# First Fourier mixer of an encoder trunk: chunk-wise shift, a first projection block that follows the chunks, and the gate's slice of the conditioning placed two blocks later

## The chip, the cores and the metric

The kernel runs on one core of one Trainium2 chip. The time is the device time of one launch in microseconds (us). A core has five engines that take their instructions in the order of the program: TensorE (PE in the rows below, with its weight loads as PEld), VectorE (DVE), ScalarE (ACT), GpSimd (POOL) and SyncE (SP), which here issues nearly all DMA transfers.

## The reference, cut to what matters

Two layers of a mixer and a channel mixer are applied to 768 tokens (512 of one group, 256 of another, each with a conditioning vector c) of width 1024. The change touches only the first mixer of layer 0, which in the reference is:

```python
mod = (cs @ ada_w[layer] + ada_b[layer])[:, None, :]      # cs = silu(c)
sh1, sc1, g1, sh2, sc2, g2 = jnp.split(mod, 6, axis=-1)
h = rmsnorm(x, norm_mix_g[layer]) * (1.0 + sc1) + sh1
hf = h.astype(jnp.float32).reshape(bsz, s, FNET_GROUPS, FNET_GROUP_DIM)
mixed = jnp.fft.fft2(hf, axes=(1, 3), norm='ortho').real.reshape(bsz, s, d).astype(h.dtype)
y = mixed @ fnet_w + fnet_b
x = x + g1 * y
```

So a Fourier transform over the sequence and over each group of 128 features, a projection 1024 x 1024, and a gated residual. Six vectors of 1024 per sequence (scale, shift and gate of the two halves of the layer) come from one product each with a slice of `ada_w`. A shift is constant along the sequence, so the transform over the sequence puts it on frequency 0 alone.

## The kernel before, in words

The work is float32. A plain float32 matmul stands in the profile's counts as two entries, so "x24" of such rows is 12 instructions. The projections run as three float32r products (high x high, low x high, high x low): weights and activations are split into a high part (cast on ACT, `wh`, `hh`) and a low part (subtraction on DVE, `wl`, `hl`).

The first mixer handles the features in 8 chunks of 128 (KC = 8). Its steps, with their lines:

- **Slices of the conditioning** (`ada_steps`, L242 to L268). A slice is 8 loads of 512 KB into tiles `at`, of which there are three (`apool`, bufs=3), each followed by four narrow matmuls into `sm`; then a copy `av`, two transposes and an addition give `modT`. Called "a group" below: the four matmuls of one load. Slice 1 is the scale, 0 the shift, 2 the gate; 4 and 3 belong to the next half of the layer.
- **Transform over the sequence** (L709 to L725): per chunk 12 float32 matmuls into a two-bank tile `big` of a pool with three buffers, then a copy to `xt` on ACT and DVE.
- **Scale and shift** (L732 to L737): `xt` times the scale on ACT and POOL, and the shift added to the two zero frequencies on DVE. This needs slices 1 and 0, so both stand before the transforms in the program.
- **Transform over the features** (L738 to L745): two matmuls per chunk, copies to `cs_` on ACT.
- **Mixing** (L746 to L756): cosine and sine parts combined on DVE and POOL to `mx`, then split to `hh` and `hl` (L195, L196).
- **Projection** (L757 to L770): for each of 8 blocks of 128 outputs, `load_block` and 24 matmuls of 512 columns and 24 of 256 (8 chunks x 3 products), in a PSUM pool `ppr` with six banks. The residual of a block (L482) multiplies by the gate, so it needs slice 2; after each block, `advance(steps, 3)` takes three steps of slices 4 and 3. The blocks are called m0 to m7 here.

The framework's scheduler sets each engine's order from the program's order as priority, and moves later work ahead where it expects the earlier work to wait. The split weights have five buffers for `wh` and five for `wl`, each half a block; the loaded weights (`stg`) have six.

Of the kernel before, what the change touches and what calls it, by code (L numbers as in the profile page):

```python
# [12 lines left out]
F32 = mybir.dt.float32  # L13
# [7 lines left out]
P = 128  # L21
# [19 lines left out]
YW = 512  # L41
PAIRS = (1, 3, 5)
ST = 4
SGB = 3
M7 = 2
WP = 5
# [59 lines left out]
def encoder_kernel(  # L106
# [87 lines left out]
    def split_to(ah, al, src, eng=None):  # L194
        A_.copy(ah, src)  # L195
        (eng or V).tensor_tensor(al, src, ah.bitcast(F32), ALU.subtract)  # L196
# [72 lines left out]
    def ada(*args):  # L269
        for s in args[0]:  # L270
            yield from ada_steps(s, *args[1:])

    def advance(gen, n=1000):
        for _ in range(n):
            if next(gen, gen) is gen:
                break
# [379 lines left out]
    with ExitStack() as l0:  # L656
# [5 lines left out]
        weights["av"] = l0.enter_context(tc.tile_pool(name="avp", reuse_waits="tile", bufs=1))  # L662
        ap0 = l0.enter_context(ExitStack())
        apool = ap0.enter_context(tc.tile_pool(name="apool", reuse_waits="tile", bufs=3))
        with ExitStack() as fs:
            pbig = fs.enter_context(tc.tile_pool(name="pbig0", reuse_waits="tile", bufs=3, space=PSUM))
            fp = fs.enter_context(tc.tile_pool(name="fp", reuse_waits="tile", bufs=1))
            wk = fs.enter_context(tc.tile_pool(name="fwk", reuse_waits="tile", bufs=2))
            ld, *rows = load_rows(wk)
            pairs = ((0, 2), (1, 3), (4, 5))  # L670
            xt = [fp.tile([P, D], F32, name="xt", bufs=8) for j in range(NT)]
            ftab = fp.tile([P, FCOLS], F32, name="ftab")
            for i, pair in enumerate(pairs):
                for j in pair:
                    nc.sync.dma_start(xt[j], x_prompt[0, j * P : (j + 1) * P, :] if j < 4 else x_sample[0, (j - 4) * P : (j - 3) * P, :])
                if i == 0:
                    nc.sync.dma_start(ftab, tab_d[:, :FCOLS])
            even = [fp.tile([P, D], F32, name=f"even{i}") for i in range(3)]
            odd = [fp.tile([P, D], F32, name=f"odd{i}") for i in range(3)]
            for i, (a, b) in enumerate(pairs):  # L680
                ss = wk.tile([P, 2], F32, name="ss")
                with tc.issue_after(ld.ins):
                    for n, (j, scratch) in enumerate(((a, even[i]), (b, odd[i]))):
                        A_.activation(scratch, xt[j], AF.Square, accum_out=ss[:, n : n + 1])
                    A_.activation(ss, ss, AF.Ln, bias=eps, scale=1.0 / D)
                    A_.activation(ss, ss, AF.Exp, scale=-0.5)
                xb = odd[i]
                V.tensor_scalar(xb, xt[b], ss[:, 1:2], None, ALU.mult)
                V.scalar_tensor_tensor(even[i], xt[a], ss[:, 0:1], xb, ALU.mult, ALU.add)
                V.scalar_tensor_tensor(odd[i], xt[a], ss[:, 0:1], xb, ALU.mult, ALU.subtract)  # L690
                for j in (a, b):
                    pt = pbig.tile([P, 1024], F32, name="big")
                    for c in range(KC):
                        last = nc.tensor.transpose(pt[:, c * P : (c + 1) * P], xt[j][:, c * P : (c + 1) * P], ident)
                    (XC[j] and A_.copy or V.tensor_copy)(xa[:, :, j * P : (j + 1) * P], pt.rearrange("p (c i) -> p c i", i=P))
                if i == 0:
                    with tc.issue_after(last.ins):
                        setup_c(psm, rows[0])
            with tc.issue_after(last.ins):
                setup_rows(psm, *rows[1:])  # L700

            NC, NS = S0 // 2 + S1 // 2 + 2, S0 // 2 + S1 // 2 - 2
            pcs = []
            advance(ada((1,), psm, apool))
            make_amod(0)
            advance(ada((0,), psm, apool))
            for c in range(KC):
                pcs.append(fp.tile([P, NC + NS], F32, name="xt", bufs=8))
                ps = pbig.tile([P, 1024], F32, name="big")  # L709
                oc, os_ = 0, 512  # L710
                for g, s in ((0, S0), (1, S1)):
                    for par in (0, 1):
                        ncs = s // 4 + 1 - par
                        nsn = s // 2 - ncs
                        nkt = s // 2 // P
                        for kt in range(nkt):
                            o, n = COLS[f"seq{g}_{kt}_{par}"]
                            src = (odd if par else even)[2 if g else kt][:, c * P : (c + 1) * P]
                            fl = dict(start=(kt == 0), stop=(kt == nkt - 1))
                            mm(ps[:, oc : oc + ncs], src, ftab[:, o : o + ncs], **fl)  # L720
                            mm(ps[:, os_ : os_ + nsn], src, ftab[:, o + ncs : o + n], **fl)
                        oc += ncs
                        os_ += nsn
                A_.copy(pcs[c][:, :NC], ps[:, :NC])
                V.tensor_copy(pcs[c][:, NC:], ps[:, 512 : 512 + NS])  # L725
            shs = fp.tile([P, KC, 2], F32, name="shs")
            for g, s in ((0, S0), (1, S1)):
                V.tensor_scalar(shs[:, :, g : g + 1], modT[:, 0, :, g : g + 1], float(s / math.sqrt(s * P)), None, ALU.mult)

            c1, s1 = S0 // 2 + 1, NC + S0 // 2 - 1  # L730
            for c in range(KC):
                y = pcs[c]  # L732
                for g, (lo, hi) in enumerate(((0, c1), (c1, NC))):
                    A_.activation(y[:, lo:hi], y[:, lo:hi], AF.Copy, scale=amod[:, 0, c, g : g + 1])
                for g, (lo, hi) in enumerate(((NC, s1), (s1, NC + NS))):
                    G.tensor_scalar(y[:, lo:hi], y[:, lo:hi], amod[:, 0, c, g : g + 1], None, ALU.mult)
                V.tensor_tensor(y[:, 0 : c1 + 1 : c1], y[:, 0 : c1 + 1 : c1], shs[:, c], ALU.add)  # L737
                pf = pbig.tile([P, 1024], F32, name="big")  # L738
                o, n = COLS["cosd"]
                mm(pf[:, 0:NC], ftab[:, o : o + n], y[:, :NC])  # L740
                o, n = COLS["sind"]
                mm(pf[:, 512 : 512 + NS], ftab[:, o : o + n], y[:, NC:])
                cs_ = wk.tile([P, NC + NS], F32, name="cs_")
                A_.copy(cs_[:, NC:], pf[:, 512 : 512 + NS])
                A_.copy(cs_[:, :NC], pf[:, :NC])  # L745
                mx = wk.tile([P, T], F32, name="mx")  # L746
                for lo, s, ec, es in ((0, S0, 0, NC), (S0, S1, c1, s1)):
                    q, h = s // 4, s // 2
                    V.tensor_copy(mx[:, lo : lo + h + 1 : h], cs_[:, ec : ec + q + 1 : q])
                    for eng, op, ev, od in (  # L750
                        (V, ALU.subtract, slice(lo + 2, lo + h, 2), slice(lo + 1, lo + h, 2)),
                        (G, ALU.add, slice(lo + s - 2, lo + h, -2), slice(lo + s - 1, lo + h, -2)),
                    ):
                        eng.tensor_tensor(mx[:, ev], cs_[:, ec + 1 : ec + q], cs_[:, es : es + q - 1], op)
                        eng.tensor_tensor(mx[:, od], cs_[:, ec + q + 1 : ec + h + 1], cs_[:, es + q - 1 : es + h - 1], op)
                split_to(hh[c], hl[c], mx)  # L756
        with ExitStack() as fs:  # L757
            fp = fs.enter_context(tc.tile_pool(name="fp2", reuse_waits="tile", bufs=1))
            ppr = fs.enter_context(tc.tile_pool(name="ppr0", reuse_waits="tile", bufs=6, space=PSUM))
            advance(ada((2,), psm, apool))  # L760
            steps = ada((4, 3), psm, apool)
            gb = fp.tile([P, KC, 2], F32, name="gb")
            V.tensor_tensor(gb, modT[:, 2], gT[:, 40:48].unsqueeze(2).to_broadcast([P, KC, 2]), ALU.mult)
            for m in range(KC):
                po = product(ppr, load_block(fnet_w[0], 0, KC, m * P), hh, hl, KC)
                for g, (lo, ln) in enumerate(SEGS):
                    A_.activation(xs[m][:, lo : lo + ln], xs[m][:, lo : lo + ln], AF.Identity, bias=gb[:, m, g : g + 1])
                residual(xs[m], po, 2, m)
                advance(steps, 3)
        ap0.close()  # L770
        with ExitStack() as fs:
            wk = fs.enter_context(tc.tile_pool(name="wk0", reuse_waits="tile", bufs=1))
# [586 lines left out]
```

## Time and profile before

| | us |
|---|---|
| median of 3 timed runs | 1894.94 (1893.63 to 1900.61) |
| the profiled execution's own time | 1897.02 |
| its span, first to last instruction | 1895.30 |
| PE busy | 1803.9 (95%) |
| DVE busy | 1422.9 (75%) |
| ACT busy | 975.1 (51%) |
| POOL busy | 501.5 (26%) |
| mean granted TensorE clock | 0.989 of full speed |

The chain that ended last is 66% PE over the span. The first mixer takes the first 156 us: slices and sequence transforms until 52.7 us, feature transforms and mixing until 75.0 us, the eight blocks after that. A granted clock of 1.00 is the higher of TensorE's two levels (2.4 GHz), 0.50 the lower (1.2 GHz).

### The profile page before, as it was taken

How to read it: one execution, taken by the hardware profiler on the slowest of the kernel's cores; microseconds unless marked ns; L12 is line 12 of the kernel's file. 1: busy time of each engine (PE TensorE's matmuls, PEld its weight loads, DVE VectorE, ACT ScalarE, POOL GpSimd, SP SyncE). 2: the span in 40 equal slices, each digit the busy share in tenths (PEclk: the TensorE clock that was granted, in tenths of full speed). 3: DMA queues.
4: the chain of work that ended last, by engine and by line, in shares of the span. 5: the costliest groups of instructions: out<-in, count | busy, mean ns of one | idle time of the engine just before them, and what ended most of it. 6: DMA issues, size and time to landing. Idle time of an engine off the chain costs nothing.

```text
span 1895.3 us, 29959 instructions
## 1 busy us (share of the span) xinstructions
PE 1803.9 (95%) x11317; PEld 1642.6 (87%) x11317; DVE 1422.9 (75%) x2431; ACT 975.1 (51%) x1863; POOL 501.5 (26%) x417
## 2 busy tenths in 40 slices
PE   8899899999999999999999999989899999999998
PEld 6587888999999987888888888778699999999997
DVE  4637777777686767897787787783788888889875
ACT  3626544444454435856666556652564554555543
POOL 1400132333332320123213213221103334343431
PEclk9999999999999999999999999999899999999999
DMA  8842344343434344322222221141312222222211
GB/s 275 245 168 67 123 134 131 109 139 110 147 112 156 112 153 151 116 51 64 64 53 66 68 64 58 53 150 39 86 34 83 84 68 68 67 70 82 72 45 67
DMA packets 221546, 189.72 MB, mean 100 GB/s; under 512 B 19152, under 2 KB 199513, under 8 KB 221401
## 3 DMA queue, kind: packets, MB, share of 16 engines
q1 hardware_dynamic: 220992, 187.66, 32.4%
q8 instruction: 89, 1.46, 0.3%
q14 instruction: 56, 0.46, 0.1%
q10 hardware_dynamic: 409, 0.15, 0.0%
HBM read 174.36 MB, written 13.42 MB: 99 GB/s over the span
## 4 chain that ended last, share of the span: by engine, by line
PE 66%; DVE 14%; ACT 6%; DMA 6%; issue 4%; POOL 3%; SPq 0%; DVEq 0%; ACTq 0%; POOLq 0%
PE pr L128 55%; PE sm L128 8%; DVE wa L957 3%; DMA stg<-in_ffn_w_gu_dram 2%; PE ax L128 1%; DVE wl L148 1%; ACT wh L147 1%; PE big L128 1%; DMA cc<-solved 1%; DVE x L561 1%; DVE wl L526 1%; POOL yy L1202 1%; POOL stg L387 1%; POOL s L387 1%; DMA stg<-in_ffn_w_down_dram 1%
## 5 line engine op out<-in xcount | busy, mean ns | idle before, releaser
L128 PE MATMUL pr<-hh,wh 128*128 128x384 f32 (+2 forms) x1520 | 520.8, 346 | 13.7 <-ACT cs__676 L745 5.3
L128 PE MATMUL pr<-hl,wh 128*128 128x384 f32 (+2 forms) x1520 | 517.8, 341 | 0.9 <-DVE hl L196 0.6
L128 PE MATMUL pr<-hh,wl 128*128 128x384 f32 (+2 forms) x1520 | 517.0, 341 | 0.7 <-DVE wl L148 0.7
L147 ACT CAST wh<-stg 128x512 fp32r<-128x512 f32 (+1 forms) x376 | 226.3, 609 | 365.7 <-PE pr L128 253.8
L148 DVE TENSOR_TENSOR wl<-stg,wh 128x512 fp32r<-128x512 f32 (+1 forms) x376 | 293.9, 787 | 102.8 <-ACT wh L147 96.6
L128 PEld LDWEIGHTS pr<-hh,wh 128*128 128x128 f32 x1520 | 286.0, 189 | 39.5 <-ACT cs__676 L745 5.8
L128 PEld LDWEIGHTS pr<-hl,wh 128*128 128x128 f32 x1520 | 286.9, 189 | 17.4 <-DVE hl L329 1.2
L128 PEld LDWEIGHTS pr<-hh,wl 128*128 128x128 f32 x1520 | 286.3, 189 | 17.8 <-DVE wl L148 1.1
L128 PE MATMUL pr<-g,wh 128*128 128x384 f32 (+2 forms) x1072 | 274.8, 338 | 7.9 <-DVE x L561 7.9
L128 PEld LDWEIGHTS pr<-g,wh 128*128 128x128 f32 x1072 | 193.0, 188 | 12.9 <-DVE x L561 11.1
L128 PE MATMUL pr<-eh,wh 128*128 128x384 f32 x536 | 184.1, 346 | 11.0 <-ACT eh L195 7.7
L128 PE MATMUL pr<-el,wh 128*128 128x384 f32 x536 | 183.1, 342 | 0.9 <-DVE el L196 0.9
L128 PE MATMUL pr<-eh,wl 128*128 128x384 f32 x536 | 182.4, 340 | 0.0
L128 PE MATMUL pr<-g,wl 128*128 128x384 f32 (+2 forms) x536 | 180.6, 337 | 0.0
L387 POOL TENSOR_TENSOR s<-stg 128x512 f32<-128x512 f32 x39 | 55.5, 1423 | 426.8 <-DMA stg<-in_ffn_w_gu_dram 377.5
L128 PEld LDWEIGHTS pr<-eh,wh 128*128 128x128 f32 x536 | 101.8, 190 | 19.9 <-ACT eh L195 9.0
L526 DVE TENSOR_TENSOR wl<-stg,wh 128x512 fp32r<-128x512 f32 x108 | 93.5, 867 | 32.6 <-ACT wh L525 31.9
L957 DVE SCALAR_TENSOR_TENSOR wa<-pad,cwT,wa 128x770 f32<-128x770 f32 x96 | 109.3, 1139 | 4.9 <-ACT wa L954 3.6
L525 ACT CAST wh<-stg 128x512 fp32r<-128x512 f32 x108 | 66.9, 621 | 80.4 <-PE pr L128 62.7
L128 PEld LDWEIGHTS pr<-el,wh 128*128 128x128 f32 x536 | 102.4, 191 | 2.5 <-DVE el L196 2.5
L128 PEld LDWEIGHTS pr<-eh,wl 128*128 128x128 f32 x536 | 102.1, 191 | 0.0
L128 PEld LDWEIGHTS pr<-g,wl 128*128 128x128 f32 x536 | 100.5, 188 | 0.7
(372 smaller groups left out, 3142.3 us busy)
## 6 DMA issues: line engine op xcount, KB each, us to landing
stg<-in_ffn_w_gu_dram SPq DMA_DIRECT2D x88, 512.0 KB, 4.1
stg<-in_ada_w_dram SPq DMA_DIRECT2D x56, 512.0 KB, 4.9
at<-in_ada_w_dram SPq DMA_DIRECT2D x40, 512.0 KB, 4.9
stg<-in_ffn_w_down_dram SPq DMA_DIRECT2D x36, 512.0 KB, 4.1
stg<-in_gdn_w_in_dram SPq DMA_DIRECT2D x33, 512.0 KB, 4.1
stg<-in_final_ada_w_dram SPq DMA_DIRECT2D x16, 512.0 KB, 7.4
raw<-gcd SPq DMA_DIRECT2D x8, 768.0 KB, 4.1
stg<-in_fnet_w_dram SPq DMA_DIRECT2D x8, 512.0 KB, 7.8
```

Of the source, the lines that this page charges most:

```text
L128: return nc.tensor.matmul(out, lhsT, rhs, start=start, stop=stop, **kw)
L147: A_.copy(wh[:, :n], src)
L148: V.tensor_tensor(wl[:, :n], src, wh[:, :n].bitcast(F32), ALU.subtract)
L387: eng.tensor_tensor(out, a, b, op)
L525: A_.copy(wh, src)
L526: V.tensor_tensor(wl, src, wh.bitcast(F32), ALU.subtract)
L561: V.scalar_tensor_tensor(x, ps[:, a - o : b - o], modT[:, gate, m, g : g + 1], x, ALU.mult, ALU.add)
L957: V.scalar_tensor_tensor(acc, pad[:, d : d + T + 2], wc[d], acc, ALU.mult, ALU.add)
L1202: G.tensor_tensor(so, so, sq, ALU.add)
```

## The change

What it does, part by part:

1. **The shift leaves the transforms.** The shift is no longer added to `xt`. It is taken through the feature transform by itself, as one small matmul (`shs`, 16 columns) with the cosine table, and added to the two zero frequencies of the mixed chunk: for chunks 4 to 7 in `mx` before the split, for chunks 0 to 3 in a small tile `first`, whose two columns are split again and written over `hh` and `hl` once the shift is there. Slice 0 stands in the program behind the feature transform of chunk 0.
2. **Chunk by chunk.** Sequence transforms of chunks 0 to 3 come first (AHEAD = 4); then each feature transform follows the sequence transform four chunks on. For chunks 4 to 7 the scale is applied while the tile is copied out of PSUM, on ACT and DVE, and not in a pass of its own on ACT and POOL.
3. **Block m0 advances with the mixed chunks.** Its weights are loaded behind chunk 0, and its two column ranges go through each chunk together, in two banks of a new pool `pf0`; `big` gives these up (two buffers of two banks in place of three).
4. **Slice 2 two blocks later.** Blocks m1 and m2 stand in the program ahead of slice 2, of the residuals of m0 to m2, and of the nine steps of slices 4 and 3 that go with them.

```diff
+AHEAD = 4
...
             advance(ada((1,), psm, apool))
             make_amod(0)
-            advance(ada((0,), psm, apool))
-            for c in range(KC):
...
-                A_.copy(pcs[c][:, :NC], ps[:, :NC])
-                V.tensor_copy(pcs[c][:, NC:], ps[:, 512 : 512 + NS])
+                if c < AHEAD:
+                    A_.copy(y[:, :NC], ps[:, :NC])
+                    V.tensor_copy(y[:, NC:], ps[:, 512 : 512 + NS])
+                    for (lo, hi), a in zip(cuts[0], scales):
+                        A_.activation(y[:, lo:hi], y[:, lo:hi], AF.Copy, scale=a)
+                    for (lo, hi), a in zip(cuts[1], scales):
+                        G.tensor_scalar(y[:, lo:hi], y[:, lo:hi], a, None, ALU.mult)
+                else:
+                    for (lo, hi), a in zip(cuts[0], scales):
+                        A_.activation(y[:, lo:hi], ps[:, lo:hi], AF.Copy, scale=a)
+                    for (lo, hi), a in zip(cuts[1], scales):
+                        V.tensor_scalar(y[:, lo:hi], ps[:, lo + 512 - NC : hi + 512 - NC], a, None, ALU.mult)
...
-                V.tensor_tensor(y[:, 0 : c1 + 1 : c1], y[:, 0 : c1 + 1 : c1], shs[:, c], ALU.add)
...
+            for c in range(AHEAD):
+                sequence(c)
+            for c in range(KC):
+                if c + AHEAD < KC:
+                    sequence(c + AHEAD)
+                features(c)
+                if c == 0:
+                    w0 = load_block(fnet_w[0], 0, KC, 0)
+
+                    advance(ada((0,), psm, apool))
...
+                    mm(pt[:, : 2 * KC], ftab[:, o : o + n], shs.rearrange("p c g -> p (c g)"))
...
+                if c == AHEAD - 1:
+                    for c in range(AHEAD):
+                        V.tensor_tensor(first[:, c], first[:, c], shs[:, c], ALU.add)
+                        split_to(hh[c][:, 0 : S0 + 1 : S0], hl[c][:, 0 : S0 + 1 : S0], first[:, c])
+
+            po0 = [bank(pf0, g)[:, :ln] for g, (_, ln) in enumerate(SEGS)]
+            for _ in zip(*(passes(ps, w0, [a[:, lo : lo + ln] for a in hh], [a[:, lo : lo + ln] for a in hl], skip_group_check=True)
+                           for ps, (lo, ln) in zip(po0, SEGS))):
+                pass
...
+            pos = [po0, projected(1), projected(2)]
             advance(ada((2,), psm, apool))
             steps = ada((4, 3), psm, apool)
...
+            for m, po in enumerate(pos):
+                added(m, po)
+            for m in range(3, KC):
+                added(m, projected(m))
```

How the built order moves, at three places. First TensorE at the start of the sequence transforms, before (`sm<-at` is a group of a slice, `big<-ftab,even` the first matmul of a chunk):

```order
L237 MATMUL sm<-ident,rows_139 128x120
L128 MATMUL sm<-at,csT 32x256 x4
L128 MATMUL big<-ftab,even_155 128x129
L128 MATMUL big<-ftab,even_155 128x127
L128 MATMUL big<-ftab,even_156 128x129
L128 MATMUL big<-ftab,even_156 128x127
L128 MATMUL sm<-at,csT 32x256 x4
```

and now:

```order
L238 MATMUL sm<-ident,rows_142 128x120
L129 MATMUL sm<-at,csT 32x256 x16
L129 MATMUL big<-ftab,even_158 128x129
L129 MATMUL big<-ftab,even_158 128x127
L129 MATMUL big<-ftab,even_159 128x129
```

The first transform now stands behind four groups of slice 1, not behind one. Second, TensorE around slice 2. Before, between the last feature transforms and block m0 (`pr<-hh_71` is the projection with chunk 0):

```order
L128 MATMUL sm<-at,csT 32x256 x4
L128 MATMUL big<-xt,ftab 128x386
L128 MATMUL big<-xt,ftab 128x382
L128 MATMUL big<-xt,ftab 128x386
L128 MATMUL big<-xt,ftab 128x382
L128 MATMUL sm<-at,csT 32x256 x11
L128 MATMUL pr<-hh_71,wh 128x512
L128 MATMUL pr<-hl_79,wh 128x512
L128 MATMUL sm<-at,csT 32x256 x4
```

and now, between the last matmul of block m2 and the first of m3:

```order
L129 MATMUL pr<-hh_78,wl 128x256
L129 MATMUL sm<-at,csT 32x256 x29
L261 MATMUL sm<-ident,av 128x128 x2
L129 MATMUL sm<-at,csT 32x256 x8
L129 MATMUL pr<-hh_71,wh 128x512
L129 MATMUL pr<-hl_79,wh 128x512
L129 MATMUL pr<-hh_71,wl 128x512
L129 MATMUL pr<-hh_72,wh 128x512
L129 MATMUL pr<-hl_80,wh 128x512
L129 MATMUL sm<-at,csT 32x256 x4
```

Of slice 2, 29 of 32 matmuls stand there in one piece (the other three stand behind the feature transform of chunk 3), then its transposes and two groups of slice 4; the other six groups of slice 4 stand inside m3, at most every fifth matmul. Third, SyncE's queue of loads. Before, from the slices on:

```order
L250 DMA at<-in_ada_w_dram 128x1024 x19
L157 DMA stg<-in_fnet_w_dram 128x8x128 x5
L250 DMA at<-in_ada_w_dram 128x1024 x3
L157 DMA stg<-in_fnet_w_dram 128x8x128 x2
L250 DMA at<-in_ada_w_dram 128x1024 x5
L157 DMA stg<-in_fnet_w_dram 128x8x128
L157 DMA stg<-in_ffn_w_gu_dram 128x8x128
L250 DMA at<-in_ada_w_dram 128x1024 x3
```

and now:

```order
L251 DMA at<-in_ada_w_dram 128x1024 x8
L158 DMA stg<-in_fnet_w_dram 128x8x128
L251 DMA at<-in_ada_w_dram 128x1024 x3
L158 DMA stg<-in_fnet_w_dram 128x8x128 x4
L251 DMA at<-in_ada_w_dram 128x1024 x8
L158 DMA stg<-in_fnet_w_dram 128x8x128 x3
L158 DMA stg<-in_ffn_w_gu_dram 128x8x128 x2
L251 DMA stg<-in_ada_w_dram 128x1024
L251 DMA at<-in_ada_w_dram 128x1024 x16
```

The second eight `at` loads are five of slice 0 and the first three of slice 2. The fourth load of slice 2 opens the row of sixteen, behind all fnet weights, two weight loads of the channel mixer and one load for a later slice.

## Rows read from the trace of the kernel before

**Rows 1.** Stretches: length, then busy us (count) by engine, TensorE clock, DMA share, GB/s

```profile
core 0: us, PE busy (x) PEld busy (x) DVE busy (x) ACT busy (x) POOL busy (x), PEclk, DMA share, GB/s
8.60:12.00 3.40, 1.66 (x13) 1.17 (x12) 1.76 (x4) 3.35 (x8) 0.00 (x0) 1.00 1.04 366
12.00:15.40 3.40, 3.40 (x17) 3.03 (x18) 2.41 (x3) 1.49 (x5) 0.00 (x0) 0.51 0.99 375
17.00:31.70 14.70, 13.21 (x126) 8.70 (x127) 10.83 (x14) 3.62 (x8) 0.00 (x0) 1.00 0.77 249
52.70:75.00 22.30, 15.05 (x82) 7.38 (x81) 20.45 (x56) 15.99 (x31) 14.64 (x31) 0.97 0.99 293
75.00:80.30 5.30, 5.27 (x23) 2.41 (x23) 3.06 (x8) 0.83 (x1) 1.96 (x4) 0.50 0.32 99
80.30:108.70 28.40, 28.40 (x207) 22.73 (x203) 9.23 (x17) 13.61 (x25) 0.00 (x0) 1.00 0.56 187
```

**Rows 2.** Waits of TensorE, 16 to 109 us: total us, times, longest

```profile
PE pr L128 <- ACT cs__676 L745: 5.3, 1, 5.3
PE sm L128 <- DMA at<-in_ada_w_dram: 2.4, 3, 1.4
PE big L128 <- ACT cs__532 L745: 0.6, 1, 0.6
```

**Rows 3.** Timeline of TensorE, 16 to 35 us: start, us, what, count [idle before]

```profile
16.92 0.64 PE L128 MATMUL sm<-at,csT 128*32 128x256 f32 x8
17.68 0.68 PE L128 MATMUL big<-ftab,even 128*128 128x129 f32 x4
...
31.13 0.64 PE L128 MATMUL sm<-at,csT 128*32 128x256 f32 x8
```

**Rows 4.** Timeline of TensorE, 52 to 80 us

```profile
52.71 5.39 PE L128 MATMUL big<-xt,ftab 128*128 128x386 f32 x16
...
64.91 0.62 PE L128 MATMUL sm<-at,csT 128*32 128x256 f32 x2 [1.43 <-DMA at<-in_ada_w_dram]
...
75.03 0.80 PE L128 MATMUL pr<-hh,wh 128*128 128x512 f32 x1 [5.29 <-ACT cs__676 L745]
```

**Rows 5.** Timeline of TensorE, 87 to 130 us

```profile
87.70 1.50 PE L128 MATMUL sm<-at,csT 128*32 128x256 f32 x24
89.13 0.50 PE L128 MATMUL pr<-hh,wh 128*128 128x512 f32 x1
...
97.72 1.50 PE L128 MATMUL sm<-at,csT 128*32 128x256 f32 x24
...
107.75 1.07 PE L128 MATMUL sm<-at,csT 128*32 128x256 f32 x16
108.75 0.50 PE L128 MATMUL pr<-hh,wh 128*128 128x512 f32 x1
...
117.28 0.38 PE L260 MATMUL sm<-ident,av 128*128 128x128 f32 x2
```

**Rows 6.** Timeline of VectorE, 48 to 78 us

```profile
51.58 0.30 DVE L737 TENSOR_TENSOR xt<-xt,shs 128x2 f32<-128x2 f32 x1 [0.28 <-ACT xt L734]
...
63.69 1.99 DVE L196 TENSOR_TENSOR hl<-mx,hh 128x768 fp32r<-128x768 f32 x2
...
68.65 1.99 DVE L196 TENSOR_TENSOR hl<-mx,hh 128x768 fp32r<-128x768 f32 x2
```

**Rows 7.** Timeline of SyncE's queue, 15 to 130 us

```profile
17.62 30.81 SPq L250 DMA_DIRECT2D at<-in_ada_w_dram  x16
```

**Rows 8.** Waits of SyncE's queue, 0 to 170 us

```profile
SPq L250 <- PE sm L128: 38.8, 28, 4.2
```

**Rows 9.** Tile `at`, 0 to 160 us: its 40 loads, issue to landing

```profile
DMA to landing us min/median/max: 4.1/4.9/7.3
```

More of the change, by code (lines that the diff above doesn't have):

```diff
@@ L664, in encoder_kernel @@
         apool = ap0.enter_context(tc.tile_pool(name="apool", reuse_waits="tile", bufs=3))
+        pf0 = ap0.enter_context(tc.tile_pool(name="pf0", reuse_waits="tile", bufs=2, space=PSUM))
         with ExitStack() as fs:
-            pbig = fs.enter_context(tc.tile_pool(name="pbig0", reuse_waits="tile", bufs=3, space=PSUM))
+            pbig = fs.enter_context(tc.tile_pool(name="pbig0", reuse_waits="tile", bufs=2, space=PSUM))
             fp = fs.enter_context(tc.tile_pool(name="fp", reuse_waits="tile", bufs=1))
@@ L705, in encoder_kernel, with sequence @@
             make_amod(0)
-            advance(ada((0,), psm, apool))
-            for c in range(KC):
-                pcs.append(fp.tile([P, NC + NS], F32, name="xt", bufs=8))
+            c1, s1 = S0 // 2 + 1, NC + S0 // 2 - 1
+            cuts = ((0, c1), (c1, NC)), ((NC, s1), (s1, NC + NS))
+            def sequence(c):
+                y = fp.tile([P, NC + NS], F32, name="xt", bufs=8)
+                pcs.append(y)
                 ps = pbig.tile([P, 1024], F32, name="big")
@@ L723, in encoder_kernel, with features @@
                         os_ += nsn
-                A_.copy(pcs[c][:, :NC], ps[:, :NC])
-                V.tensor_copy(pcs[c][:, NC:], ps[:, 512 : 512 + NS])
[L726 to L731, printed above, removed]
-                y = pcs[c]
[L733 to L736, printed above, removed]
-                V.tensor_tensor(y[:, 0 : c1 + 1 : c1], y[:, 0 : c1 + 1 : c1], shs[:, c], ALU.add)
+                scales = [amod[:, 0, c, g : g + 1] for g in range(2)]
+                if c < AHEAD:
[10 more added lines that the diff above has]
+                        V.tensor_scalar(y[:, lo:hi], ps[:, lo + 512 - NC : hi + 512 - NC], a, None, ALU.mult)
+            first = fp.tile([P, AHEAD, 2], F32, name="first")
+            def features(c):
+                y = pcs[c]
                 pf = pbig.tile([P, 1024], F32, name="big")
@@ L745, in encoder_kernel @@
                 A_.copy(cs_[:, :NC], pf[:, :NC])
+                if c < AHEAD:
+                    V.tensor_copy(first[:, c], cs_[:, 0 : c1 + 1 : c1])
                 mx = wk.tile([P, T], F32, name="mx")
@@ L755, in encoder_kernel @@
                         eng.tensor_tensor(mx[:, od], cs_[:, ec + q + 1 : ec + h + 1], cs_[:, es + q - 1 : es + h - 1], op)
+                if c >= AHEAD:
+                    V.tensor_tensor(mx[:, 0 : S0 + 1 : S0], mx[:, 0 : S0 + 1 : S0], shs[:, c], ALU.add)
                 split_to(hh[c], hl[c], mx)
+            for c in range(AHEAD):
[7 more added lines that the diff above has]
+                    advance(ada((0,), psm, apool))
+                    shs = fp.tile([P, KC, 2], F32, name="shs")
+                    for g, s in ((0, S0), (1, S1)):
+                        V.tensor_scalar(shs[:, :, g : g + 1], modT[:, 0, :, g : g + 1], float(s / math.sqrt(s * P)), None, ALU.mult)
+                    pt = psm.tile([P, 512], F32, name="sm")
+                    o, n = COLS["cosd"]
+                    mm(pt[:, : 2 * KC], ftab[:, o : o + n], shs.rearrange("p c g -> p (c g)"))
+                    V.tensor_copy(shs.rearrange("p c g -> p (c g)"), pt[:, : 2 * KC])
+                if c == AHEAD - 1:
+                    for c in range(AHEAD):
+                        V.tensor_tensor(first[:, c], first[:, c], shs[:, c], ALU.add)
+                        split_to(hh[c][:, 0 : S0 + 1 : S0], hl[c][:, 0 : S0 + 1 : S0], first[:, c])
@@ L757, in encoder_kernel @@
+            po0 = [bank(pf0, g)[:, :ln] for g, (_, ln) in enumerate(SEGS)]
+            for _ in zip(*(passes(ps, w0, [a[:, lo : lo + ln] for a in hh], [a[:, lo : lo + ln] for a in hl], skip_group_check=True)
+                           for ps, (lo, ln) in zip(po0, SEGS))):
+                pass
         with ExitStack() as fs:
             fp = fs.enter_context(tc.tile_pool(name="fp2", reuse_waits="tile", bufs=1))
-            ppr = fs.enter_context(tc.tile_pool(name="ppr0", reuse_waits="tile", bufs=6, space=PSUM))
+            ppr = fs.enter_context(tc.tile_pool(name="ppr0", reuse_waits="tile", bufs=4, space=PSUM))
@@ L760, in encoder_kernel, with projected, added @@
+            def projected(m):
+                return product(pf0 if m % 3 == 0 else ppr, load_block(fnet_w[0], 0, KC, m * P), hh, hl, KC)
+            def added(m, po):
+                for g, (lo, ln) in enumerate(SEGS):
+                    A_.activation(xs[m][:, lo : lo + ln], xs[m][:, lo : lo + ln], AF.Identity, bias=gb[:, m, g : g + 1])
+                residual(xs[m], po, 2, m)
+                advance(steps, 3)
+            pos = [po0, projected(1), projected(2)]
             advance(ada((2,), psm, apool))
@@ L763, in encoder_kernel @@
             V.tensor_tensor(gb, modT[:, 2], gT[:, 40:48].unsqueeze(2).to_broadcast([P, KC, 2]), ALU.mult)
[L764 to L769, printed above, removed]
+            for m, po in enumerate(pos):
+                added(m, po)
+            for m in range(3, KC):
+                added(m, projected(m))
         ap0.close()
```

## The prediction, made before the changed kernel ran

> **What bounds the kernel now.** I read the page's first part (TensorE busy 95% of the span), then the stretches of the first mixer [rows 1], TensorE's waits there [rows 2], its timeline, and last VectorE and SyncE's queue. The reader is to see that TensorE is the bound in most of the first 156 us, and where it isn't. Between 52.7 and 75.0 us it is busy 15.05 of 22.30 us while DVE is busy 20.45 [rows 1]: the mixing of the chunks runs on DVE at 2.48 us each (two chunks between 63.69 and 68.65) [rows 6], and m0 starts only when the last chunk's copy is out, after 5.29 us of idleness [rows 4]. Until 80.3 us TensorE then has its lower clock, 0.50 [rows 1]. From 80.3 on it is full. SyncE's queue waits mostly for TensorE to free an `at` tile (38.8 us in 28 waits) [rows 8]: with three tiles, 16 loads took 30.81 us from the first issue to the end of the last [rows 7].
>
> **What can be won.** In the stretch from 52.7 us TensorE idles 5.29 us before m0, 1.43 for a load and 0.6 for a copy [rows 2, 4]: 7.3 us. The low clock for 5.3 us costs half of it, 2.65 [rows 1]. If the joined order keeps TensorE fed, both go: 9.9 us, and this is the ceiling, since the matmuls stay the same in number but for one of 16 columns.
>
> **Cost 1: the start of the transforms.** Before, the first transform starts at 17.68 us, behind one group [rows 3]. Now it stands behind four. The fourth load can be issued only when the first group has freed its tile, at 17.62 us [rows 7], and lands a median 4.9 us later [rows 9]: 22.5, with its group 23.1. What TensorE did before from 17.0 until the eighth group ended at 31.7 was 13.2 us of work [rows 1], less four groups of some 0.57 (the pitch of a group between transforms): 10.9 left, so the same point is reached at 34.0, 2.3 us late. While it waits, TensorE is busy about a third of the time. It was busy 1.66 of 3.40 us before 12.0, and then had clock 0.51 for 3.4 us [rows 1]; if that follows here, half of 3.4 us more is lost, 1.7. I take 0.9, the middle.
>
> **Cost 2: the joined phase.** Once the last sequence transform is done, TensorE has four feature transforms (5.39 / 4 = 1.35 each) [rows 4] and eight passes of m0 (8.6 us for 24 + 24 matmuls, 89.13 to 97.72, so 1.07 each) [rows 5], 14 us in all, against four chunks of DVE work, 10 us. TensorE is the longer, but each chunk crosses ACT, DVE, ACT, DVE before its pass. The waits are between none and the 7.3 us of before; I take 1.5, nearer to none, since 14 us of work cover 10. The small edits go in here with one answer. New are twelve DVE steps on two columns and four ACT casts, and the copies of chunks 4 to 7 out of PSUM with the scale; gone are eight DVE steps of 0.30 us [rows 6] and eight POOL passes. They lie under TensorE's transforms; with that cover gone, the upper bound of this cost holds them.
>
> **Cost 3: slice 2 behind m2.** Now TensorE does m1 and m2 with no group between. In the order, 29 of slice 2's matmuls and two groups of slice 4 stand between m2 and m3. m3 cannot overtake them for a reason beyond the order: its banks are m0's, and m0's residual needs the gate.
>
> First, when m2 ends. Before, at 107.75, and m3 began at 108.75 [rows 5]. Now 9.9 earlier by the waits and the clock; 6.6 earlier because 53 narrow matmuls (29 of slice 2, 24 of slice 4's six groups that stood behind m0 and m1) and two transposes leave this part, at 1.43 us for 12 [rows 5]; 4.7 later by costs 1 and 2: 95.9 us.
>
> Then the loads. Three of slice 2 are in their tiles early. The first tile's fourth matmul opens the row of 29, so its tile is held until m2 ends, and the load that wants it waits at the head of SyncE's queue, with everything behind it. So at 95.9 seven loads (five of slice 2, two of slice 4) have yet to be issued, one at a time as tiles come free. First issue after 0.4 (its four matmuls), landing 4.9 later [rows 9]. The pace with three tiles is bounded by the rows: 2.0 us per load as in the 16 loads (30.81 less one issue, over 15) [rows 7], or, if each lands in the shortest time seen, (4.1 + 0.6) / 3 = 1.6 [rows 9]; a median landing gives 1.8. I take 1.9, nearer to the 16 loads, which are the same transfers. Six more at 1.9, the last group 0.5: m3 starts 0.4 + 4.9 + 11.4 + 0.5 = 17.2 us after m2, of which TensorE works 4.7. It starts at 113.1, 4.4 later than before.
>
> By then six groups of slice 4 are still to do that were done before: 6 x 0.48 = 2.9 us inside m3. Their loads keep the pace of 1.9, while m3 offers five matmuls of 0.24 (8.6 us over 24 of 512 columns and 24 of 256, two of these as one) and a group, 1.7 us; but m3 restarts after 12.5 us of near idleness, so I charge it the same low clock as m0 had, 2.65 [rows 1], and the slower matmuls hide the rest. After m3 TensorE's order is that of before, and the wait that follows the mixer moves along with it.
>
> The queue itself moves little else: two weight loads of the channel mixer come earlier, and one load for a later slice stands just ahead of the seven. At 512 KB and 249 to 375 GB/s [rows 1] it may cost the first landing up to 1.4 to 2 us; I keep that for the range.
>
> The Trainium skill ("DMA: Bandwidth & Descriptors", section Anatomy of one DMA) puts a transfer at about 2.0 us plus its bytes over 436 GB/s, which for 512 KB would be an estimated 3.2 us. The 40 loads here took 4.1 at the least [rows 9], so the row decides; by the page the pace would be 1.3 and the gap 11.7 us in place of 17.2.
>
> **The sum.** 4.4 + 2.9 + 2.65 = 9.9 us slower. As a ledger: won 9.9, paid 2.3 + 0.9 + 1.5 + 12.5 + 2.65 = 19.8. Against the profiled execution's own time, 1897.0 (span 1895.3 and 1.7 around it), this is 1906.9; that execution was 2.1 above the median, so on the scale of the timed runs 1894.9 + 9.9 = 1904.8 us, 0.5% slower.
>
> **The bounds.** Downward: cost 1 at nothing (-3.2), no waits in cost 2 (-1.5), first landing 4.1 and pace 1.6 (-2.6), the clock low for only 3.4 us (-0.9): +1.7, so 1896.6. Upward: cost 1 with its full clock loss (+0.8), all 7.3 us of waits kept (+5.8), a late first landing (+2), the pace not hidden in m3 (+1.5): +20, so 1915.
>
> **Rivals.** (a) *The chain of the chunks stays the bound.* DVE's work per chunk is not shortened, and it was busy 92% of that stretch [rows 1]; if the hand-overs keep TensorE waiting as before, cost 2 is 7.3 and not 1.5: 1904.8 + 5.8 = 1910.6. For it speaks the full DVE; against it that DVE starts on chunk 0 with four sequence transforms still to come.
>
> (b) *The loads run at their fastest.* Between m2 and m3 nothing else is on the DMA engines, so each could land in 4.1 us and the pace be 1.6; with the gap shorter by 2.6, the low clock shorter (-0.9) and none at the start (-0.9): +5.5, 1900.4. Against it: the three tiles in flight share the engines, and the median is 4.9. The page's rule above is this rival carried further: it gives about 1899.
>
> (c) *Slice 2 is there in time.* If the fourth load went out before m2 ended, slice 2 and its successors would load under m1 and m2 (20 us of matmuls, eight loads at 1.9 need 15), the 12.5 us of idleness and the clock behind it would not arise, and the change would win 9.9 less 4.7: 1889.7, not slower. What decides is whether the first tile of slice 2 is freed ahead of m1; in the order only three of its four matmuls stand there, so this needs the order to be other than it is.
>
> That the change does not do what it says is excluded for the order of the instructions, which the rows of the order show; it can only miss its end, as in (a).
>
> **How the numbers follow.** Forecast 0.62, (a) 0.18, (b) 0.14, (c) 0.06. Some 0.5% (9.5 us) is what a measurement of this kernel can tell from no change, so slower begins at 1904.4. The forecast lies on that bound and gives about half of its chance to each side, with (a) on the slower side: 0.32 + 0.18 = 0.50. The same: the other half, (b), and most of (c), 0.47. Faster, below 1885.5, only if (c) went at its best: 0.03. The range from 1897 to 1911 leaves out (c) and the far ends.
>
> **What would show it.** Right: TensorE's first transform at about 23 us, not 17.7; the wait before m0 gone and its matmuls at clock 1.00; m2 ending near 96 us; then a row of waits of `sm` for loads of `at`, 10 us or more in all, with SyncE's queue issuing seven loads one by one after m2; m3 starting near 113 us at the low clock. Wrong: m3 starting less than 10 us after m2 (cost 3 is mis-sized), m2 ending after 100 us (cost 2), or a first transform before 19 us (cost 1).

## The result, and the profile after

The changed kernel takes 1.0042 times the time of the kernel before (95% interval 1.0031 to 1.0054; medians 1903.95 and 1898.03 us of 14 runs each): 8.0 us slower, 5.9 to 10.2. The two medians by themselves differ by 5.9 us, the lower end of that. Forecast were 9.9. The bound of 9.5 us between "the same" and "slower" lies inside the interval, so the time alone does not choose between them; the trace shows the steps.

Seven stretches of the kernel after (length, busy us and count by engine, granted TensorE clock, DMA share, GB/s), beside [rows 1]:

```profile
17.00:22.60 5.60, 2.58 (x35) 0.91 (x34) 5.60 (x6) 2.48 (x5) 0.00 (x0) 1.00 0.68 235
22.60:25.70 3.10, 3.10 (x23) 2.06 (x19) 3.10 (x6) 0.20 (x1) 0.00 (x0) 0.55 0.82 272
25.70:68.00 42.30, 41.69 (x324) 30.37 (x321) 25.31 (x81) 19.82 (x46) 16.79 (x32) 0.99 0.85 251
68.00:93.20 25.20, 24.58 (x141) 21.04 (x139) 10.54 (x26) 7.03 (x14) 3.39 (x8) 1.00 0.15 42
93.20:110.40 17.20, 9.45 (x77) 2.48 (x76) 2.26 (x7) 2.10 (x4) 0.00 (x0) 0.64 0.81 274
110.40:135.70 25.30, 25.23 (x186) 17.06 (x186) 11.06 (x21) 12.90 (x23) 0.00 (x0) 0.97 0.71 233
135.70:163.10 27.40, 27.40 (x178) 23.00 (x178) 10.08 (x17) 5.45 (x10) 0.00 (x0) 1.00 0.34 114
```

TensorE is busy all but some 1.2 us from 22.6 to 93.2, at full clock (0.99 and 1.00) from 25.7 on: the hole ahead of m0 is gone. Two new holes stand there, one ahead of the transforms (2.58 of 5.60 us busy) and the large one from 93.2 to 110.4, where TensorE is busy 9.45 of 17.20 us at clock 0.64: its clock is 0.98 until 98.2, then, after a wait of 3.56 us, 0.50 until 111.5. In the stretch in which the end of m0, m1 and m2 run (68.0 to 93.2), the DMA engines stand at 0.15; as soon as m2 is done they go to 0.81. That is the pattern to look for: a transfer that could have run under the matmuls, and did not.

The waits of TensorE from 16 to 135 us (total us, times, longest), which answer to [rows 2]:

```profile
PE sm L129 <- DMA at<-in_ada_w_dram: 10.0, 6, 3.6
PE pr L129 <- DVE hl L197: 0.6, 1, 0.6
PE big L129 <- ACT cs__636 L755: 0.6, 1, 0.6
PE sm L261 <- DMA at<-in_ada_w_dram: 0.5, 1, 0.5
PE pr L129 <- DVE x L483: 0.2, 1, 0.2
```

The 5.3 us for ACT before m0 became 1.2 in two hand-overs; 2.4 us for loads became 10.5. TensorE's timeline shows where these stand (start, us, what, count, idle before):

```profile
93.20 1.48 PE L129 MATMUL sm<-at,csT 128*32 128x256 f32 x18
98.24 1.08 PE L129 MATMUL sm<-at,csT 128*32 128x256 f32 x8 [3.56 <-DMA at<-in_ada_w_dram]
100.44 1.08 PE L129 MATMUL sm<-at,csT 128*32 128x256 f32 x8 [1.12 <-DMA at<-in_ada_w_dram]
...
106.08 1.08 PE L129 MATMUL sm<-at,csT 128*32 128x256 f32 x8 [1.85 <-DMA at<-in_ada_w_dram]
107.71 0.69 PE L261 MATMUL sm<-ident,av 128*128 128x128 f32 x2 [0.55 <-DMA at<-in_ada_w_dram]
108.32 1.94 PE L129 MATMUL sm<-at,csT 128*32 128x256 f32 x16
110.47 0.79 PE L129 MATMUL pr<-hh,wh 128*128 128x512 f32 x1 [0.21 <-DVE x L483]
```

And SyncE's queue, beside [rows 7]:

```profile
75.97 9.17 SPq L158 DMA_DIRECT2D stg<-in_ffn_w_gu_dram  x2
93.17 0.34 SPq L251 DMA_DIRECT2D stg<-in_ada_w_dram  x1
93.86 28.97 SPq L251 DMA_DIRECT2D at<-in_ada_w_dram  x16
```

m2 ends at 93.20. Not one load of slice 2 beyond those in the tiles goes out while m1 and m2 run; the first follows 0.66 us after m2, and 16 loads then take 28.97 us. m3 starts at 110.47, 1.7 us later than before. The end of the mixer (last product of m7) is at 163.1 in place of 155.9, +7.2. Before, the row is:

```profile
155.66 0.28 PE L128 MATMUL pr<-hh,wl 128*128 128x256 f32 x1
```

This mark serves below as the meter of the trace, beside the timed ratio; the two agree within 2 us in every run. There is one trace of each version. What follows the mixer takes between 1734 and 1744 us in the 13 traces, not in step with what the mixer gains or loses (1739.4 before, 1736.4 after), and already the first group of slice 1 starts anywhere from 16.9 to 18.0 us. So a difference of about 1 us or less between two mixer's ends is not told from none.

### The profile page after: what moved, and what is told of

The parts are those of the page before. It is cut to its first block, busy times and chain, and to the rows that moved or that the text cites. A ratio compares the mean times of both kernels' runs of the same rounds, so it can differ in the third digit from the quotient of the medians.

```text
span 1899.5 us, 29963 instructions
## 1 busy us (share of the span) xinstructions
PE 1803.2 (95%) x11319; PEld 1639.7 (86%) x11319; DVE 1423.9 (75%) x2444; ACT 973.3 (51%) x1863; POOL 494.7 (26%) x409
## 4 chain that ended last, share of the span: by engine, by line
PE 68%; DVE 14%; ACT 6%; DMA 6%; issue 3%; POOL 3%; SPq 0%; DVEq 0%; ACTq 0%; POOLq 0%
PE pr L129 55%; PE sm L129 8%; DMA stg<-in_ffn_w_gu_dram 3%; DVE wa L1007 3%; PE big L129 2%; DVE wl L149 2%; PE ax L129 1%; ACT wh L148 1%; DVE x L562 1%; DMA at<-in_ada_w_dram 1%; POOL yy L1252 1%; DMA cc<-solved 1%; DVE wl L527 1%; DMA xt<-in_x_prompt_dram 1%; DMA stg<-in_ffn_w_down_dram 1%
## 5 line engine op out<-in xcount | busy, mean ns | idle before, releaser
L129 PE MATMUL pr<-hh,wh 128*128 128x384 f32 (+2 forms) x1520 | 519.4, 345 | 10.2 <-ACT up L417 3.5
L129 PEld LDWEIGHTS pr<-hh,wl 128*128 128x128 f32 x1520 | 285.7, 188 | 17.6 <-DVE wl L149 1.1
L129 PEld LDWEIGHTS pr<-g,wh 128*128 128x128 f32 x1072 | 192.9, 188 | 13.5 <-DVE x L562 11.6
L129 PE MATMUL pr<-eh,wh 128*128 128x384 f32 x536 | 183.7, 345 | 11.6 <-ACT eh L196 8.5
```

The costliest lines, as they stand in the source:

```text
L129: return nc.tensor.matmul(out, lhsT, rhs, start=start, stop=stop, **kw)
```

## The experiments

Theory: the loss is the gap behind m2, made by where slice 2 stands and by the three tiles it holds; parts 1 to 3 win a few us. Main rival: the joined order gives back what it wins, and part 4 is innocent. Each run was timed against the kernel before on its chip; us are the ratio less 1, times 1895.

| version | us against before (95%) | first transform | m2's end to m3 | mixer's end |
|---|---|---|---|---|
| before | 0 | 17.7 | 1.0 | 155.9 |
| changed | +8.0 (5.9 to 10.2) | 22.6 | 17.3 | 163.1 |
| e1 changed, without part 4 | -1.3 (-3.4 to 0.8) | 23.1 | 1.0 | 153.7 |
| e2 before, part 4 alone | +8.9 (6.3 to 11.6) | 17.8 | 12.0 | 165.6 |
| e3 changed, five tiles | +5.5 (3.2 to 7.8) | 22.9 | 13.3 | 161.3 |
| e4 before, two `big` | +2.3 (-0.2 to 4.9) | 23.2 | 1.0 | 159.2 |
| e5 changed, copies on ACT | +8.7 (5.3 to 11.9) | 17.6 | 17.8 | 162.8 |
| e6 before, copies on ACT | -2.3 (-4.2 to -0.4) | 18.8 | 1.0 | 154.8 |
| e7 slice 2 among the chunks | -4.7 (-7.2 to -2.3) | 22.9 | 1.0 | 153.2 |
| e8 = e7, five tiles, copies | -8.7 (-11.6 to -5.9) | 17.7 | 1.0 | 146.1 |
| e9 before, five tiles, copies | -2.3 (-4.2 to -0.4) | 18.6 | 1.0 | 154.3 |
| e10 = e7, five tiles | -6.1 (-8.0 to -4.0) | 22.1 | 1.0 | 148.7 |
| e11 changed, five tiles, copies | +1.1 (-0.9 to 3.2) | 17.8 | 12.1 | 157.8 |

**e1: part 4 undone.**

```diff
-            pos = [po0, projected(1), projected(2)]
             advance(ada((2,), psm, apool))
...
-            for m, po in enumerate(pos):
-                added(m, po)
-            for m in range(3, KC):
-                added(m, projected(m))
+            for m in range(KC):
+                added(m, projected(m) if m else po0)
```

> Part 4 undone in the changed kernel: slice 2 stands right behind m0's passes in the program, and each block has its residual and its three steps again; parts 1 to 3 stay. Theory (the loss is the gap behind m2, made by where slice 2 stands): m3 follows m2 with no gap, waits of sm for loads between 80 and 125 us are under 3 us in all, the mixer ends 9 to 11 us before that of the changed kernel, the time is 2 to 5 us under the kernel before (won 9.9, paid 2.3 + 1.7 at the start, 1.2 in the joined phase, about 2 for slice 2's loads behind m0). Rival 1 (the joined order itself loses what it wins, and part 4 is innocent): the time stays within 2 us of the changed kernel. Rival 2 (loads of slice 2 are slow wherever they stand): the gap moves to behind m0 with 10 us or more of waits, the time is at or above the kernel before.

The mixer ends 9.4 us before that of the changed kernel and the time falls by about as much (+8.0 to -1.3). TensorE's only wait for a load in the stretch from 60 to 125 us:

```profile
PE sm L129 <- DMA at<-in_ada_w_dram: 1.3, 1, 1.3
```

So part 4 is the loss, and rivals 1 and 2 fall. The gain over the kernel before is smaller than expected: the trace says 2.2 us, the time does not tell it from none.

**e2: part 4 alone.** The loops of the change's part 4, with all of m0 by `projected(0)`:

```diff
-            for m in range(KC):
-                po = product(ppr, load_block(fnet_w[0], 0, KC, m * P), hh, hl, KC)
+            pos = [projected(0), projected(1), projected(2)]
+            advance(ada((2,), psm, apool))
+            steps = ada((4, 3), psm, apool)
...
+            for m, po in enumerate(pos):
+                added(m, po)
+            for m in range(3, KC):
+                added(m, projected(m))
```

> The kernel before with part 4 alone: m0, m1 and m2 stand ahead of slice 2 and of the residuals of m0 to m2; the transforms, the shift and m0 stay as they were, with three big buffers. Theory: three tiles of slice 2 are held until m2 ends, and the same row of loads, one by one, opens behind m2: TensorE waits 4 to 8 us for sm there, and the time is 6 to 10 us over the kernel before. Rival 1 (the gap needs the joined order ahead of it): waits behind m2 under 3 us, time within 2 us of the kernel before.

The gap opens in the old order too; TensorE behind m2:

```profile
100.22 1.50 PE L128 MATMUL sm<-at,csT 128*32 128x256 f32 x24
106.30 2.31 PE L128 MATMUL sm<-at,csT 128*32 128x256 f32 x16 [4.58 <-DMA at<-in_ada_w_dram]
109.16 0.69 PE L260 MATMUL sm<-ident,av 128*128 128x128 f32 x2 [0.55 <-DVE av L256]
...
112.25 0.80 PE L128 MATMUL pr<-hh,wh 128*128 128x512 f32 x1
```

Part 4 costs its whole price by itself, +8.9 us, as expected.

**e3: five tiles.** `apool` with bufs=5.

> The changed kernel with five at tiles in place of three, the order of the program untouched. Theory (the loads go out one by one because the tiles are held): five of slice 2's eight loads are in place when m2 ends, so fewer loads are to be issued behind it; the gap from m2's end to m3 falls from 17.3 us to 11 to 14, the wait of 2.9 us ahead of the first transform shrinks below 1, and the time is 4 to 7 us under the changed kernel. Rival (the DMA engines are the bound, a load takes what it takes): the gap stays at 16 to 18 us and the time within 2 us of the changed kernel.

The gap falls to 13.3 us, as expected; the gain is 1.8 us by the mixer's end and 2.5 by the times, whose intervals overlap: less than the 4 to 7 expected. The start shows why:

```profile
18.81 0.64 PE L129 MATMUL sm<-at,csT 128*32 128x256 f32 x8 [0.54 <-DMA at<-in_ada_w_dram]
20.05 0.64 PE L129 MATMUL sm<-at,csT 128*32 128x256 f32 x8 [0.60 <-DMA at<-in_ada_w_dram]
22.88 1.44 PE L129 MATMUL big<-ftab,even 128*128 128x129 f32 x5 [2.19 <-DVE x L697]
```

The loads are now in time, and the first transform starts no earlier: it waits for DVE's copy of the transposed input out of `big` (in the changed kernel DVE begins these copies at 21.15 us). There this wait hid behind a load that came at about the same time. The low clock behind the start lasts longer besides, 0.50 from 22.9 to 27.0 us and 0.71 from there to 30.0, where the changed kernel has 0.55 for 3.1 us and then the full clock. With that and 0.7 us more of waits, m2 ends at 94.85, 1.65 us later than in the changed kernel, and this takes its part of the 4.0 us that the gap gains.

**e4: two `big` buffers in the kernel before.** `pbig0` with bufs=2.

> The kernel before with two big buffers in place of three, nothing else. Theory (the late first transform comes from the third buffer that part 3 takes away): the first transform stands behind four groups and starts at 22 to 23 us in place of 17.7, with 3.4 us of low clock there; what is lost at the start is 3 to 4 us, some of it covered by the wait before m0, so the time is 0 to 4 us over the kernel before. Rival (the late start comes from the shift's move, part 1, which puts slice 0 behind the first feature transform): the first transform stays at 17 to 18 us and the time within 1 us of the kernel before, or over it only by waits between transforms.

TensorE at the first transform:

```profile
22.10 0.64 PE L128 MATMUL sm<-at,csT 128*32 128x256 f32 x8 [2.38 <-DMA at<-in_ada_w_dram]
23.18 1.23 PE L128 MATMUL big<-ftab,even 128*128 128x129 f32 x4 [0.44 <-DVE x L695]
```

And DVE's copies that free the buffers:

```profile
21.91 2.35 DVE L695 COPY x<-big 128x1024 f32<-128x1024 f32 x2
```

The buffer alone moves the start from 17.7 to 23.2. The time, +2.3, is within the expected range and only just not told from none; the mixer's end says +3.3.

**e5: the two copies on ACT, in the changed kernel.**

```diff
-XC = (0, 0, 0, 0, 0, 0)
+XC = (0, 0, 0, 0, 1, 1)
```

> The changed kernel with the two PSUM copies of the last pair of input tiles (x out of big, ahead of the transforms) on ACT in place of DVE, nothing else. Theory (the first transform is late because both big buffers wait for these copies, which DVE does only after 21 us; the wait for the fourth load of at only ends at about the same time and hides this): one group stands ahead of the first transform, which starts at 17 to 19 us at full clock, and the time is 2 to 4 us under the changed kernel; the gap behind m2 stays at 16 to 18 us. Rival (the prediction's reason: the fourth load is the wait): the first transform stays at 21 us or later and the time within 1 us of the changed kernel.

The cause of the late start is right, its price wrong. ACT copies early:

```profile
15.60 1.95 ACT L697 COPY x<-big 128x1024 f32<-128x1024 f32 x2 [2.06 <-PE big L696]
```

And TensorE starts the transforms on time:

```profile
17.63 1.13 PE L129 MATMUL big<-ftab,even 128*128 128x129 f32 x8
```

Yet m2 ends only 1.6 us earlier (91.6), since 3.5 us of waits stand between 17 and 92, where the changed kernel had 1.2 beside the one of 2.9; and of the 1.6 the mixer's end shows 0.3: the gap takes 0.5 more, and from m3 to the mixer's end it takes 0.7 more. The time shows no gain.

**e6: the same copies in the kernel before.**

> The kernel before with the same two copies on ACT; three big buffers. Theory (the third buffer covers these copies, so that only DVE's chain gains, by up to 2.35 us): the first transform stays at 17 to 18 us, the time is 0 to 4 us under the kernel before, and the gain is smaller than that of the same edit in the changed kernel. Rival (the copies gain the same wherever they are, and have nothing to do with the third buffer): 2 to 4 us in both.

-2.3 us (1.1 by the mixer's end), inside the expected range. The first transform starts at 18.8 and not at 17 to 18; it waits 0.89 us for DVE's `even`. That the edit gains less here than in the changed kernel is not borne out: there neither the time nor the mixer's end shows a gain. The intervals are too wide to show that it gains more here.

**e7: slice 2 ahead of the mixing of the last chunk**, on e1:

```diff
                 features(c)
...
+                if c == KC - 2:
+                    advance(ada((2,), psm, apool))
```

> Parts 1 to 3 with slice 2 placed ahead of the mixing of the last chunk, so that its loads run under the feature transforms and m0's passes; residuals and steps go with each block as before the change; copies and tiles as in the changed kernel. Theory: no group of slice 2 is left behind m0, waits of sm between 60 and 125 us are under 2 us, m1 follows m0 with a gap under 2 us, and the time is 2 to 6 us under the kernel before, 1 to 3 under the changed kernel without part 4. Rival (the joined phase has no room: m0's passes are pushed out by as much as the groups take): the time equals that of the changed kernel without part 4 within 1 us.

-4.7 us, as the theory had it, and faster than the kernel before. Against e1 the trace gives 0.5 us at the mixer's end, which is no more than the rival allows; the times say more, but their intervals overlap. What the place among the chunks is worth over that of e1 is not shown. Waits for loads were 2.3 us and not under 2, and the pause between m0 and m1 2.8 us and not under 2.

**e8: e7 with five tiles and the copies on ACT.**

> Slice 2 ahead of the mixing of the last chunk, the two copies on ACT and five at tiles together, on parts 1 to 3. Theory (start, gap and loads are separate losses, so their cures add up): the first transform at 17 to 19 us, m0's passes done before 79 us, the mixer's end 6 to 9 us before that of the kernel before, and the time 5 to 9 us under it. Rival (the cures overlap, or the time is given back behind the mixer): 0 to 4 us under it.

-8.7 us, the fastest of all by its ratio, with its interval clear of both kernels. The mixer ends 9.8 us before that of the kernel before, more than the 6 to 9 expected. All its waits of TensorE from 16 to 135 us, and then its stretches up to 98:

```profile
PE sm L261 <- DVE av L257: 1.4, 1, 1.4
PE big L129 <- DVE even L691: 0.3, 1, 0.3
```

```profile
17.00:30.00 13.00, 12.57 (x123) 8.35 (x123) 8.84 (x12) 5.48 (x11) 0.00 (x0) 1.00 0.97 349
30.00:66.40 36.40, 36.30 (x295) 24.80 (x292) 22.70 (x78) 17.80 (x43) 16.43 (x32) 1.00 0.77 258
66.40:78.00 11.60, 10.24 (x64) 7.80 (x66) 8.54 (x27) 8.21 (x17) 3.45 (x8) 1.00 0.97 313
78.00:98.00 20.00, 20.00 (x148) 16.04 (x144) 6.36 (x10) 8.42 (x16) 0.00 (x0) 1.00 0.74 237
```

No wait for a load is left, TensorE's clock is full in these rows, and the DMA engines work under m0 to m2 (0.97 from 66.4 to 78.0, 0.74 from there to 98.0; the changed kernel shows 0.15 from 68.0 to 93.2).

**e9: both cures in the kernel before**, the control for e8.

> The kernel before with the two copies on ACT and five at tiles, without parts 1 to 4. Theory (parts 1 to 3 win by keeping TensorE fed between the transforms and m0, which neither cure does): TensorE still waits 3 to 6 us before m0 and has its low clock in m0; the mixer's end is 3 to 5 us before that of the kernel before and 5 us or more behind that of the version with slice 2 ahead of the last chunk, the copies on ACT and five tiles; the time is 2 to 4 us under the kernel before. Rival (the gain of that version comes from copies and tiles alone): 7 to 10 us under it.

```profile
PE pr L128 <- ACT cs__676 L745: 5.0, 1, 5.0
```

The wait before m0 stays, as expected; the mixer's end gains 1.6 us (3 to 5 expected), the time 2.3. So the cures alone are not what e8 gains: its mixer, with parts 1 to 3 and slice 2 among the chunks, ends 8.2 us before that of e9.

**e10: e7 with five tiles, copies on DVE.**

> The version with slice 2 ahead of the last chunk's mixing with five at tiles, copies on DVE. Theory (with the loads in time the late start is the only loss left): first transform at 22 to 24 us, no wait for loads over 1 us after it, the mixer's end 1 to 3 us before that of the same version with three tiles and 3 us or more behind that with the copies on ACT too; the time 4 to 7 us under the kernel before. Rival (the copies add nothing here either, as in the changed kernel): within 1 us of the version with both cures, 7 to 10 us under the kernel before.

The mixer ends 4.5 us before that of e7, more than expected, and 2.6 behind e8, a little under the 3 expected. The times of e8 and e10 overlap; which is faster rests on the trace alone.

**e11: both cures, part 4 kept.**

> The changed kernel, part 4 kept, with both cures: the two copies on ACT and five at tiles. Theory (behind m2 the row of loads is the bound, so a gain ahead of it arrives in full only as far as TensorE's m2 ends earlier): the first transform at 17 to 19 us, m2's end at 88 to 92, the gap 11 to 14 us, the mixer's end 0 to 3 us behind that of the kernel before and 7 us or more behind the version with slice 2 ahead of the last chunk; the time 0 to 3 us over the kernel before. Rival (with the cures part 4 costs nothing): the time 7 us or more under the kernel before.

As expected in each point. The gap with five tiles:

```profile
91.95 2.37 PE L129 MATMUL sm<-at,csT 128*32 128x256 f32 x40
98.37 1.08 PE L129 MATMUL sm<-at,csT 128*32 128x256 f32 x8 [4.05 <-DMA at<-in_ada_w_dram]
```

Five groups are in place, the sixth waits 4 us as ever: its load goes out only when m2 is over. Against e8, which has slice 2 among the chunks, e11 still ends its mixer 11.7 us later. The cures give 0.3 us (copies) and 1.8 (tiles) apart, and 5.3 together; the five tiles alone keep the late start, the copies alone keep the long gap. That this is all of the 5.3 is argued and not shown.

## Why the prediction was right, step by step

- **What is won.** Right. The wait before m0 and the low clock in it are gone (clock 1.00 from 68.0 to 93.2).
- **Cost 1, the late first transform.** 22.6 where 23.1 was forecast, and the clock lost in full (0.55 over 3.1 us, some 1.4 us, where the prediction took 0.9). The reason given, the fourth load, is only half of it, so that the start came out so near is in part luck: e3 took the load's wait away and the start stayed; e4 made it late, and e5 early, by the buffer and its copies alone. The price was too high as well: with the start on time m2 ends 1.6 us earlier (e5, among new waits for loads), or the mixer 2.6 us earlier where the loads are in time (e10 to e8), not 3.2 or more.
- **Cost 2, the joined phase.** 1.2 us of waits, 1.5 forecast. Rival (a) falls.
- **m2's end.** 93.2, forecast 95.9. From 17.5 us to m2's end TensorE's idle time fell by 4.5 us (8.77 to 4.26), where the prediction's terms make 3.5 (7.3 - 2.3 - 1.5); its busy time fell by 10.0 (81.48 to 71.44), where they make 8.35 (2.65 + 6.6 - 0.9). The mis-sized term is the work that leaves this part. The groups from the transforms to m2's end, before (17.5 to 107.9 us) and after (17.5 to 93.2):

```profile
L128 PE MATMUL sm<-at,csT 128*32 128x256 f32 x240 | 19.7, 402 | 2.4 <-DMA at<-in_ada_w_dram 2.4
```

```profile
L129 PE MATMUL sm<-at,csT 128*32 128x256 f32 x134 | 10.7, 403 | 3.0 <-DMA at<-in_ada_w_dram 2.9
```

  These are 9.0 us in their own rows, where the prediction had 6.6 with the transposes. It priced a group at 0.48 us from a row of twelve matmuls back to back (1.43 us); one by itself among wide matmuls costs more, as m3 shows below.
- **Cost 3, the gap.** 17.3 us, forecast 17.2: one load at a time, as told. TensorE is busy 9.45 us of it and not 4.7, since its groups run at the low clock there (1.08 us each); the loads' pace hides that. The loads' median in the profile after is 4.8 us (`at`, x40, 512 KB), so rival (b), with 14.6, falls; (c) falls with the order. The Trainium skill ("DMA: Bandwidth & Descriptors", Anatomy of one DMA) gives its figure for transfers that GpSimd issues, and these are SyncE's; the 11.7 us estimated from it is not what the trace shows. Beside this, the reading of [rows 8] in the prediction's first paragraph holds only until 80 us (33.6 us of waits for TensorE); over the whole window SyncE's queue waits longer, 64.0 us, for DVE's `wl`. No term rests on it.
- **m3 and after.** From m3's start to the mixer's end 52.6 us against 47.2, so some 5.5 longer; 2.9 + 2.65 = 5.55 was forecast. That the sum is so near is luck, since both terms were wrong. The stretch of m3 and m4, before (108.7 to 128.5 us):

```profile
L128 PE MATMUL pr<-hh,wh 128*128 128x512 f32 x16 | 6.5, 408 | 0.0
...
L128 PE MATMUL sm<-at,csT 128*32 128x256 f32 x44 | 3.0, 383 | 0.0
```

  and after (110.4 to 135.7):

```profile
L129 PE MATMUL pr<-hh,wh 128*128 128x512 f32 x16 | 6.9, 432 | 0.2 <-DVE x L483 0.2
...
L129 PE MATMUL sm<-at,csT 128*32 128x256 f32 x88 | 6.6, 389 | 0.0
```

  The groups' rows are 3.6 us longer and those of the wide matmuls some 1.4, 0.4 of it in the row shown. The low clock has little part in it: it is 0.50 from m3's start to 111.5 us and 0.94 from there to 113.0, which costs some 0.6 us and not 2.65. A group by itself costs more than was charged:

```profile
113.97 0.40 PE L129 MATMUL pr<-hh,wh 128*128 128x512 f32 x1
114.30 0.64 PE L129 MATMUL sm<-at,csT 128*32 128x256 f32 x8
114.87 0.50 PE L129 MATMUL pr<-hl,wh 128*128 128x512 f32 x1
115.21 0.40 PE L129 MATMUL pr<-hh,wl 128*128 128x512 f32 x1
```

  From 113.97 to 115.21 pass 1.24 us for a group and two wide matmuls, which take 0.23 each, from start to start, where no group is near. So the group costs 0.77 and not 0.48, and the six in m3 an estimated 4.6 us and not 2.9.
- **The sum.** +7.2 at the mixer's end and +8.0 timed, 9.9 forecast; the difference is m2's end. The prediction held "slower" (0.50) and "the same" (0.47) for nearly equal; the measured 8.0 lies on the side of the second, with an interval that reaches over the bound.

So the mechanism and the largest term held; the smaller ones erred in both directions and in part cancelled.

## What to carry to other kernels

Work that is put later in program order takes its loads along: they start only when a tile comes free, so a step that is moved behind a long stretch of matmuls is paid for in transfers that could have run under it (DMA share 0.15, then 0.81). Place the first use of a rotating tile early, among the work that is to hide its loads, and look at the share of the DMA engines under the longest matmul stretch. Where a wait is named for one releaser, take it away before you believe its price: a second one (a PSUM buffer not yet copied out) may end at the same time, and what the cure wins may only reach the next wait.

## What was not expected of the hardware

A group of four narrow matmuls among wide ones costs more than its share of a row: 0.64 us at full clock where it stands alone, against 1.07 for two and 1.50 for three in a row, so an estimated 0.43 for each further one. It slows its neighbours too, so that in m3 it cost 0.77 from start to start. And more tiles do not speed up the first load: behind m2 TensorE waits for it 3.6 to 4.6 us with three tiles (changed kernel 3.56, e5 4.29, e2 4.58) and 4.1 with five (e3 4.11, e11 4.05).
